# An encoder layer on one core: h's plain block through DRAM, T1 and T2 queued ahead, a tile pair of their own for w_down's first digits, the last store in halves

## The chip, the cores and the metric

The kernel runs on one core of one Trainium2 chip. The metric is the device time of one execution in microseconds (us); lower is better. Before the change three runs took 1528.82 to 1530.57 us, median 1529.31.

Engines are named as in the profile: PE is TensorE's matmul and PEld its weight load, DVE is VectorE, ACT is ScalarE, POOL is GpSimd, SP is SyncE, which here only issues DMAs. A DMA can be issued from ACT too (ACTq).

## The reference, cut to what matters

One layer on x of 1024 tokens by 1024 channels, all in float32:

```
h = rmsnorm(x, g_mix)
... pooling mixer and differential attention on h @ w_in, two gates ...
x = x + merged @ w_out
h2 = rmsnorm(x, g_ffn)
x = x + square(relu(h2 @ w_up)) @ w_down      # w_up: 1024 x 4096, w_down: 4096 x 1024
```

The change lies in the last three lines: the product with `w_out` (its end), the second norm, and the two products of the MLP.

## The kernel before

**Float32 out of three matmuls.** Every operand of a matmul is kept as two digits: `split` (L129-133) casts a block to hi on ACT (L131) and subtracts to get lo on DVE or POOL (L132). `mm3` (L135-140) then makes one product of 128 x 128 by 128 x 512 from three matmuls: hi x hi (L138), hi x lo (L139), lo x hi (L140).

**Seven products in place of eight.** The large products are cut into 2 x 2 blocks and done by a scheme of seven block products, named "1" to "7", with sums of blocks as operands. For w_up the token side is h2 transposed, in blocks B11, B21 (tokens 0 to 511, lower and upper half of the channels) and B12, B22 (tokens 512 to 1023). The operands are B11, B21, B22 and

```
T1 = B12 - B11      T2 = B22 - T1      T3 = B22 - B12      T4 = (B21 - B11) - T3
```

Each has a hi and a lo tile, filled in four column blocks of 128 tokens (t = 4 to 7). The profile names them BT1h, BT1l and so on; "t" is a block of T1 or T2 before the cast, "y" the block of h2 itself.

**End of the w_out stage, `first_half` (L1151-1159).** For tokens t = 0 to 3 the normed block is transposed on PE into two banks (hb) and split into B11 and B21. A plain copy of B11 (`r11`, ACT) is subtracted from B21, and the difference d21 is stored to DRAM (`nd`, SP), where T4 needs it later. r11 and d21 come from `tmp`, four slots in turn.

**The turn to the MLP, `second_half` and `combine` (L1272-1299).** For t = 4 to 7 the block is transposed and scaled by ACT (L1178) into `kept_b[t]`, which holds B12 and B22. T1 is made by two subtractions on DVE, B12 minus B11's hi and minus its lo; then T2 by one. T2 is split at once; T1, T3, B22 and T4 are split by four calls of `combine`, in this order. `combine("T3")` and `("22")` also work within y's room; for T4 the stored d21 is loaded back over B22 (L1297) once B22 is split.

**w_up, `up_pair` (L1332-1407).** Sixteen pairs p of column blocks; each pair has seven products of 12 matmuls: "1" on B11 into bank X, "2" on B21 into Y, then "6" (T2), "5" (T1), "7" (T3), "4" (T4), "3" (B22). The first products of pairs 0 to 3 run ahead during the turn. The second half of a pair's columns (`wu<p>_1`) is loaded into `pr20` or `pr21`; pr21 lies where the y blocks lay. The results go to DRAM (`ud`) as they are and in four sums us1 to us4 (udS), made last in each pair.

**w_down (L1458-1594).** Seven products of eight steps q; a step is 24 matmuls on two operands of 128 x 1024: `ur`, loaded back from ud, and a sum of blocks of w_down (`wd`, `wdt`). `operands` loads both and splits them into u_q and w_q. Those of product "1" for q = 0 to 2 are made early, beside the last pair; `t1_made(q)` makes T1 of w_down from `wdt` and gives back the tile of step q. At the end `finish_out` adds the bank to what was kept and stores four blocks of 128 x 512.

**What sets the order.** Each engine works through its own queue in order. The order of each queue isn't written by hand: a planner puts an instruction into its queue when, by its own estimates, its operands and its room are there, the most urgent by priority (`tc.cur_priority`) first. `tc.issue_after(x)` puts what is traced within it behind x in the queue of x's engine, without a wait. Waits are then added where data or a tile's bytes need them.

**Room.** Tiles are drawn from pools that are stacked from both sides of a partition, and pools of a later stage lie over closed ones of an earlier stage. The byte ranges per partition in the last two stages are these.

| w_up stage | bytes | w_down stage | bytes |
|---|---|---|---|
| wpool (cast w_up) | 18176-50944 | pwo (w digits) | 18176-50944 |
| hpT2, T1, T3, 22, T4 | 50944-132864 | pd (T1, T2, kept sums, residuals) | 50944-147200 |
| e1 (9 blocks: t, x1, U2, z5, U3, us) | 132864-151296 | prw1 (4 wd tiles) | 155392-171776 |
| es | 151296-155392 | pur1 (2 ur tiles) | 171776-179968 |
| e21 (s of other pairs) | 155392-163584 | puo (8 u digits) | 179968-212736 |
| pr21, e20, pr20 | 163584-179968 | prw0 (2 wd tiles) | 212736-220928 |
| pr1 (w_up) | 179968-196352 | pur0 (2 ur tiles) | 220928-229120 |
| nb (B11, B21) | 196352-229120 | | |

e1 itself lies over `rpool` and `fp` of the stage before it, where the raw w_out rows and `tmp`'s blocks are.

Of the kernel before, what the change touches and what calls it, by code (L numbers as in the profile page):

```python
# [8 lines left out]
F32 = mybir.dt.float32  # L9
# [8 lines left out]
P = 128  # L18
S = 1024
D = 1024  # L20
NT = S // P
# [42 lines left out]
def encoder_kernel(  # L64
# [21 lines left out]
    nc = tc.nc  # L86
    x, out = x[0], out[0]
# [5 lines left out]
    dram = ctx.enter_context(tc.tile_pool(name="dram", bufs=1, space=DRAM))  # L93
# [32 lines left out]
    def f(ap):  # L126
        return ap.bitcast(F32)

    def split(hi, lo, src, lo_eng=None):  # L129

        made = nc.scalar.copy(hi, src)  # L131
        (lo_eng or nc.vector).tensor_tensor(lo, src, f(hi), op=ALU.subtract)  # L132
        return made
# [264 lines left out]
    def fillers():  # L398
        gate_units = gates()
        for _ in range(G_FIRST):  # L400
            next(gate_units)
            yield
        for g in range(4):
            for _ in pool_group(g):
                yield
                next(gate_units)
                yield
        for _ in gate_units:
            yield
# [3 lines left out]
    with ExitStack() as ph:  # L413
# [83 lines left out]
        act, dve, pol = nc.scalar, nc.vector, nc.gpsimd  # L497
# [426 lines left out]
        units, made = fillers(), 0  # L924
# [29 lines left out]
    def add(eng, out_, a, b):  # L954
        eng.tensor_tensor(out_, a, b, op=ALU.add)

    def sub(eng, out_, a, b):
        eng.tensor_tensor(out_, a, b, op=ALU.subtract)

    dve, pool = nc.vector, nc.gpsimd  # L960
# [22 lines left out]
    def tmp(name):  # L983
        nbank[1] += 1
        return fr_tile([P, 512], name) if nbank[1] % 4 in (1, 2) else fo_tile(name)[:, 0:512]
# [22 lines left out]
    for d in range(NK):  # L1008
        if d % 2 == 0 and d + 2 < NK:
            ws_bp[d + 2] = load_cols2(w_branch_pool, (d + 2) * P, f"bp{d + 2}")  # L1010
        elif d > NK - 4:
            j = len(ws_ba)
# [126 lines left out]
    def norm_turn(t, bank_fn):  # L1139

        yn = y[t]
        ps = [bank_fn(j, f"hb{t}_{j}") for j in range(2)]
        for j, b in enumerate(ps):
            for i in range(4):
                k = 4 * j + i
                nc.tensor.transpose(b[:, i * P : (i + 1) * P], yn[:, k * P : (k + 1) * P], identf)
        return [b.rearrange("p (a b) -> p a b", a=4) for b in ps]

    nd = dram.tile([4, P, 4, P], F32, name="nd")

    def first_half(t):  # L1151
        b11, b21 = norm_turn(t, lambda j, name: o_bank(name, 2 * (t % 2) + j))
        b_split("11", t * P, b11, dve)
        b_split("21", t * P, b21, dve)

        r11, d21 = (tmp(f"{n}_{t}").rearrange("p (a b) -> p a b", a=4) for n in ("r11", "d21"))
        nc.scalar.copy(r11, b11)
        sub(dve, d21, b21, r11)
        nc.sync.dma_start(nd[t], d21)


    def o_bank(name, i):
        p, tag = ((ps_z, "z"), (ps_z, "z"), (ps_f, "f"), (pb, "b"))[i]
        return p.tile([P, 512], F32, tag=tag, name=name)

    kept_b, turned = {}, {}
# [6 lines left out]
    def second_turn(t, b):  # L1173
        kept_b[t] = y[t].rearrange("p (q a b) -> p q a b", q=2, a=4)
        for j in range(2):
            for i in range(4):
                k = 4 * j + i
                turned[t] = nc.scalar.activation(  # L1178
                    kept_b[t][:, j, i, :], b[j][:, i, :], AF.Copy, scale=cols[:, 21 + k : 22 + k]
                )  # L1180
# [47 lines left out]
    for step in O_TAIL.split():  # L1228
        t = int(step[1])
# [34 lines left out]
    def ev(name, shape=(P, 512)):  # L1264
        return e1.tile(list(shape), F32, tag="ev", name=name)
# [1 line left out]
    for q in ("T2", "T1", "T3", "22", "T4"):  # L1267
        Bq[q] = tuple(hpT[q].tile([P, 4, 512], F32R, tag="h", name=f"B{q}{i}") for i in "hl")

    T1s, T2_made = {}, {}  # L1270

    def second_half(t, after=None):  # L1272
        c0 = (t - 4) * P
        if after is not None:
            with tc.issue_after(after.ins):
                second_turn(t, norm_turn(t, lambda j, name: bm.tile([P, 512], F32, tag="ZW"[j], name=name)))
        t1, t2 = (ev(f"{n}_{t}", (P, 4, P)) for n in ("t1", "t2"))
        T1s[t] = t1
        cs = slice(c0, c0 + P)
        sub(dve, t1, kept_b[t][:, 0], f(Bq["11"][0][:, :, cs]))  # L1280
        sub(dve, t1, t1, f(Bq["11"][1][:, :, cs]))
        sub(dve, t2, kept_b[t][:, 1], t1)
        T2_made[t] = b_split("T2", c0, t2, dve)

    def combine(q):
        for t in range(4, NT):
            c0 = (t - 4) * P
            t3, b22 = kept_b[t][:, 0], kept_b[t][:, 1]
            if q == "T1":
                b_split(q, c0, T1s[t], dve)  # L1290
            elif q == "T3":
                sub(dve, t3, b22, t3)
                b_split(q, c0, t3, dve)
            elif q == "22":
                b_split(q, c0, b22, dve)
            else:
                nc.sync.dma_start(b22, nd[t - 4])  # L1297
                sub(dve, b22, b22, t3)
                b_split(q, c0, b22, dve)
# [14 lines left out]
    made = {}  # L1314
# [108 lines left out]
    for p, q in enumerate(("T1", "T3", "22", "T4")):  # L1423
        if p > 1:
            next(pairs[p])
        if q == "T3":
            body = tc.cur_priority

        with ExitStack() as later:
            if p:  # L1430
                later.enter_context(tc.issue_after(turned[NT - 1].ins))
            if q == "T4":
                later.enter_context(tc.issue_after(T2_made[NT - 1].ins))
            combine(q)
    norms.close()
    e2 = [pool_of(hs, "e20", 2, side="right")]
# [18 lines left out]

    purs = [pool_of(ctx, "pur0", 2, side="right")]  # L1458
    prws = [pool_of(ctx, "prw0", 2, side="right")]
    puo = pool_of(ctx, "puo", 8, side="right")  # L1460
# [3 lines left out]
    pwo = pool_of(ctx, "pwo", 8)  # L1464
# [4 lines left out]
    T1s, T2s = {}, {}  # L1469

    def kept(tag, q):
        return pd.tile([P, 2, 512], F32, tag=tag, name=f"{tag}_{q}", bufs=NQ)
# [4 lines left out]
    def quarter(j, q, ab, dh):  # L1477
        nraw[1] += j not in "1t"
        first = q % 4 < 2 if j == "1" else j != "t" and nraw[1] % 3 == 0
        r = prws[0 if first else 1].tile([P, 2, 512], F32, tag="rw", name=f"wd{j}_{q}_{ab}{dh}")  # L1480
        nc.sync.dma_start(r, wd[ab, :, q, :, dh * 512 : (dh + 1) * 512])
        return r

    def second(j, q):

        if j == "1":
            b11[q] = quarter(j, q, 0, 0)
            return b11[q]
        if j == "5":
            return T1s[q]  # L1490
        if j == "2":
            return quarter(j, q, 1, 0)
        if j == "3":
            return quarter(j, q, 1, 1)
        if j == "6":
            b22 = quarter(j, q, 1, 1)
            T2s[q] = kept("T2", q)
            sub(dve, T2s[q], b22, T1s[q])
            return T2s[q]
        if j == "7":  # L1500
            b22, b12 = quarter(j, q, 1, 1), quarter(j, q, 0, 1)
            sub(dve, b22, b22, b12)
            return b22
        b21 = quarter(j, q, 1, 0)
        sub(dve, b21, b21, T2s[q])
        return b21
# [3 lines left out]
    def t1_made(q):  # L1510
        b12 = quarter("t", q, 0, 1)
        T1s[q] = kept("T1", q)
        sub(dve, T1s[q], b12, b11.pop(q))

    def operands(j, q):
        nraw[0] += 1
        ur = purs[nraw[0] > 2 and nraw[0] % 2].tile([P, 2, 512], F32, tag="ur", name=f"ur{j}_{q}")
        nc.sync.dma_start(ur, ud[SIDES[j][0], q])
        out_ = []
        for n, src, pool_ in (("u", ur, puo), ("w", second(j, q), pwo)):  # L1520
            hi, lo = (pool_.tile([P, 2, 512], F32R, tag="op", name=f"{n}{j}_{q}{x}") for x in "hl")
            split(hi, lo, src, dve)
            out_ += [hi, lo]
        return out_

# [35 lines left out]
            got.append(k)  # L1561
        return got

    def finish_out(banks, parts, th, dh):
        for t in range(4):
            add(dve, parts[t], banks[t], parts[t])
            r0 = (4 * th + t) * P
            nc.sync.dma_start(out[r0 : r0 + P, dh * 512 : (dh + 1) * 512], parts[t])

    def four(tag):  # L1570
        return [bd.tile([P, 512], F32, tag=tag, name=f"D{tag}{t}", bufs=4) for t in range(4)]
# [16 lines left out]
    U3 = with_residual(DX, "U3y", 1, 0)  # L1588
# [2 lines left out]
    finish_out(DZ, U2, 0, 1)  # L1591
    DV = four("a")
    d_product(DV, "4", True)
    finish_out(DV, U3, 1, 0)


# [29 lines left out]
```

## Time and profile before

| | |
|---|---|
| three runs | 1529.31 us median, 1528.82 to 1530.57 |
| the profiled execution | 1529.07 us, of which the profile's span is 1527.3 |
| PE busy | 1518.3 us, 99% of the span, 7638 matmuls |
| DVE, ACT, POOL busy | 1018.6, 803.3, 357.6 us |
| DMA | 213.75 MB, mean 140 GB/s |
| granted TensorE clock | 1.00 |

The profile is one execution. Its span begins with the first recorded work and ends with the last; the 1.8 us between the span and the execution's time lie around it. A row of a timeline gives start and length in us, the engine, the line of the code, the operation, the output and the inputs, and in brackets how long the engine stood idle before it and what ended that. A matmul is shown with 0.39 us though the next starts 0.23 us later, since matmuls are pipelined; a PE that is "busy" can thus still lose time, which shows in the distance of starts. A row of busy time in a stretch gives, after the stretch, the busy us and the number of instructions of PE, PEld, DVE, ACT and POOL, then the granted clock, the DMA engines' busy share and GB/s. The row of a DMA issue ends with its size and the us from issue to landing. By time, w_out ends and the turn to the MLP begins at 905 us, w_up runs to 1217 and w_down to the end.

### The profile page before, as it was taken

How to read it: one execution, taken by the hardware profiler on the slowest of the kernel's cores; microseconds unless marked ns; L12 is line 12 of the kernel's file. 1: busy time of each engine (PE TensorE's matmuls, PEld its weight loads, DVE VectorE, ACT ScalarE, POOL GpSimd, SP SyncE). 2: the span in 40 equal slices, each digit the busy share in tenths (PEclk: the TensorE clock that was granted, in tenths of full speed). 3: DMA queues.
4: the chain of work that ended last, by engine and by line, in shares of the span. 5: the costliest groups of instructions: out<-in, count | busy, mean ns of one | idle time of the engine just before them, and what ended most of it. 6: DMA issues, size and time to landing. Idle time of an engine off the chain costs nothing.

```text
span 1527.3 us, 21610 instructions
## 1 busy us (share of the span) xinstructions
PE 1518.3 (99%) x7638; PEld 1316.7 (86%) x7638; DVE 1018.6 (67%) x2073; ACT 803.3 (53%) x1653; POOL 357.6 (23%) x403
## 2 busy tenths in 40 slices
PE   9999999999999999999999999999999999999999
PEld 8999999999999999888888887888888788888887
DVE  7777766677676777642745899676656678556572
ACT  6656565556565655544633467565555634333331
POOL 4424142424233342227736510000000000000000
PEclk9999999999999999999999999999999999999999
DMA  6212121111212021339845633554432899537750
GB/s 219 65 44 66 36 63 38 59 52 47 62 36 75 31 90 49 118 108 357 280 144 176 211 137 118 173 193 159 152 124 110 290 332 365 185 125 262 225 194 28
DMA packets 168583, 213.75 MB, mean 140 GB/s; under 512 B 10165, under 2 KB 104090, under 8 KB 168474
## 3 DMA queue, kind: packets, MB, share of 16 engines
q1 hardware_dynamic: 151050, 185.05, 36.6%
q10 hardware_dynamic: 17424, 27.31, 4.8%
q8 instruction: 60, 0.98, 0.3%
q14 instruction: 49, 0.40, 0.1%
HBM read 154.62 MB, written 57.70 MB: 139 GB/s over the span
## 4 chain that ended last, share of the span: by engine, by line
PE 93%; DVE 4%; DMA 1%; ACT 1%; issue 1%; SPq 0%; POOLq 0%; POOL 0%; ACTq 0%; DVEq 0%
PE z L138 6%; PE z L140 6%; PE z L139 6%; PE Da L139 4%; PE Da L140 4%; PE g L139 4%; PE Da L138 4%; PE g L140 4%; PE g L138 4%; PE Db L140 3%; PE Db L138 3%; PE Db L139 3%; PE X L138 3%; PE X L140 3%; PE X L139 3%; PE sc L774 2%
## 5 line engine op out<-in xcount | busy, mean ns | idle before, releaser
L138 PE MATMUL z<-wqkv,hT 128*128 128x384 f32 x512 | 174.2, 341 | 0.1
L140 PE MATMUL z<-wqkv,hT 128*128 128x384 f32 x512 | 174.0, 340 | 0.3 <-DVE hT L437 0.3
L139 PE MATMUL z<-wqkv,hT 128*128 128x384 f32 x512 | 173.1, 338 | 0.0
L785 ACT ACTIVATE s<-s,nm 128x256 f32<-128x256 f32 (+7 forms) x128 | 99.5, 778 | 73.3 <-DVE nm L777 72.6
L708 POOL TENSOR_TENSOR ms<-ms,mhalf 128x4 f32<-128x4 f32 x64 | 70.6, 1103 | 210.3 <-DVE ms L707 207.1
L139 PE MATMUL g<-hT,fwgate 128*128 128x512 f32 x256 | 100.7, 394 | 0.0
L138 PE MATMUL g<-hT,fwgate 128*128 128x512 f32 x256 | 100.7, 393 | 0.0
L140 PE MATMUL g<-hT,fwgate 128*128 128x512 f32 x256 | 100.5, 394 | 0.0
L138 PEld LDWEIGHTS z<-wqkv,hT 128*128 128x128 f32 x512 | 96.2, 188 | 3.3 <-ACT hT L437 0.4
L139 PEld LDWEIGHTS z<-wqkv,hT 128*128 128x128 f32 x512 | 96.3, 188 | 2.5 <-DVE wqkv L437 0.3
L140 PEld LDWEIGHTS z<-wqkv,hT 128*128 128x128 f32 x512 | 96.2, 188 | 2.5 <-DVE hT L437 0.8
L777 DVE CUSTOM_DVE_ANT_0 s<-sc,dist 128x512 f32<-128x512 f32 (+3 forms) x128 | 74.6, 586 | 22.9 <-PE sc L775 21.7
L774 PE MATMUL sc<-K,Q 128*128 128x512 f32 (+2 forms) x192 | 67.6, 356 | 0.1
L775 PE MATMUL sc<-K,Q 128*128 128x512 f32 (+2 forms) x192 | 65.7, 348 | 0.0
L132 DVE TENSOR_TENSOR AS<-s,AS 128x512 fp32r<-128x512 f32 x64 | 43.4, 687 | 32.4 <-ACT AS L131 32.3
L132 POOL TENSOR_TENSOR wqkv<-rqkv,wqkv 128x384 fp32r<-128x384 f32 x56 | 58.1, 1062 | 11.8 <-ACT wqkv L131 11.3
L132 POOL TENSOR_TENSOR fwgate<-frgate,fwgate 128x512 fp32r<-128x512 f32 x32 | 44.5, 1392 | 69.1 <-ACT fwgate L131 69.1
L140 PEld LDWEIGHTS g<-hT,fwgate 128*128 128x128 f32 x256 | 48.1, 188 | 9.6
L139 PEld LDWEIGHTS g<-hT,fwgate 128*128 128x128 f32 x256 | 48.1, 188 | 9.0 <-DVE hT L132 0.3
L138 PEld LDWEIGHTS g<-hT,fwgate 128*128 128x128 f32 x256 | 48.1, 188 | 8.8 <-ACT hT L131 0.3
L132 DVE TENSOR_TENSOR AT_0l<-ta,AT_0h 128x512 fp32r<-128x512 f32 (+1 forms) x48 | 32.0, 666 | 30.9 <-ACT AT_0h L131 30.4
L138 PE MATMUL ba<-yT,wba 128*128 128x512 f32 x128 | 49.8, 389 | 0.0
(484 smaller groups left out, 4583.6 us busy)
## 6 DMA issues: line engine op xcount, KB each, us to landing
wd<-in_w_down_dram SPq DMA_DIRECT2D x56, 512.0 KB, 5.5
wu<-in_w_up_dram SPq DMA_DIRECT2D x32, 512.0 KB, 4.3
udS<-us SPq DMA_DIRECT2D x64, 256.0 KB, 3.4
ur<-udS SPq DMA_DIRECT2D x32, 512.0 KB, 5.3
rqkv<-in_w_in_dram SPq DMA_DIRECT2D x64, 192.0 KB, 2.7
ur<-ud SPq DMA_DIRECT2D x24, 512.0 KB, 5.7
frgate<-in_w_gate_dram SPq DMA_DIRECT2D x32, 256.0 KB, 3.8
g_dram<-go ACTq DMA_DIRECT2D x32, 256.0 KB, 2.5
```

The lines of the kernel that those rows point to most:

```text
L132: (lo_eng or nc.vector).tensor_tensor(lo, src, f(hi), op=ALU.subtract)
L138: nc.tensor.matmul(ps, lhs_hi, rhs_hi, start=first, stop=False, **kw)
L139: nc.tensor.matmul(ps, lhs_hi, rhs_lo, start=False, stop=False, **kw)
L140: return nc.tensor.matmul(ps, lhs_lo, rhs_hi, start=False, stop=last, **kw)
L708: nc.gpsimd.tensor_tensor(ms, ms, mhalf[:, 0:4], op=ALU.pow)
L774: nc.tensor.matmul(dst, Q[:, i, 0, :], rhs, start=True, stop=False)
L775: nc.tensor.matmul(dst, Q[:, i, 1, :], rhs, start=False, stop=True)
L777: nc.vector.tensor_tensor_reduce(out=s[i][:, c : c + w], in0=sc[:, 0:w], in1=dist[:, o0 + c : o0 + c + w], scale=2.0 ** -(h + 1), scalar=B ...
L785: nc.scalar.activation(s[i][:, 0:n], s[i][:, 0:n], AF.Exp, bias=last, scale=-1.0, accum_out=Z[:, i, t : t + 1])
```

## The change

- **nr.** `first_half` also stores r11, the plain block of B11, to DRAM (`nr`, SP). Before the turn four loads bring the blocks back into the tiles that will be T1. T1 is then one subtraction, B12 minus the loaded block, in place of two.
- **Order.** What `combine` casts for T3, B22 and T4 is now queued on ACT behind the casts of the last block (t = 7) of T2 and of T1; before, it was queued behind the last turned block, and T4 behind T2 too.
- **pw0.** A pool of two tiles (8 KB), opened first on the right side, takes the two digits w_0 of product "1"; all others stay in pwo. The ACT casts of u and w for q = 2 and 3 of product "1" are queued behind w_0's cast.
- **Last store.** The last block of the last product is added and stored in two halves of 256 columns, the first store on SP, the second on ACT.

```diff
-    nd = dram.tile([4, P, 4, P], F32, name="nd")
+    nd, nr = (dram.tile([4, P, 4, P], F32, name=n) for n in ("nd", "nr"))
...
         nc.scalar.copy(r11, b11)
+        nc.sync.dma_start(nr[t], r11)
         sub(dve, d21, b21, r11)
...
-    T1s, T2_made = {}, {}
+    T1s, T2_made, T1_made = {}, {}, {}
+    for t in range(4, NT):
+        T1s[t] = ev(f"t1_{t}", (P, 4, P))
+        nc.sync.dma_start(T1s[t], nr[t - 4])
...
-        t1, t2 = (ev(f"{n}_{t}", (P, 4, P)) for n in ("t1", "t2"))
-        T1s[t] = t1
-        cs = slice(c0, c0 + P)
-        sub(dve, t1, kept_b[t][:, 0], f(Bq["11"][0][:, :, cs]))
-        sub(dve, t1, t1, f(Bq["11"][1][:, :, cs]))
+        t1, t2 = T1s[t], ev(f"t2_{t}", (P, 4, P))
+        sub(dve, t1, kept_b[t][:, 0], t1)
         sub(dve, t2, kept_b[t][:, 1], t1)
...
             if q == "T1":
-                b_split(q, c0, T1s[t], dve)
+                T1_made[t] = b_split(q, c0, T1s[t], dve)
...
             if p:
-                later.enter_context(tc.issue_after(turned[NT - 1].ins))
-            if q == "T4":
                 later.enter_context(tc.issue_after(T2_made[NT - 1].ins))
+                later.enter_context(tc.issue_after(T1_made[NT - 1].ins))
             combine(q)
...
+    pw0 = pool_of(ctx, "pw0", 2, side="right")
     purs = [pool_of(ctx, "pur0", 2, side="right")]
...
+        first = (j, q) == ("1", 0)
+        for n, src, pool_ in (("u", ur, puo), ("w", second(j, q), pw0 if first else pwo)):
             hi, lo = (pool_.tile([P, 2, 512], F32R, tag="op", name=f"{n}{j}_{q}{x}") for x in "hl")
-            split(hi, lo, src, dve)
+            with tc.issue_after(first_w[0].ins) if j == "1" and 1 < q < 4 else nullcontext():
+                made = split(hi, lo, src, dve)
+            if first:
+                first_w[0] = made
...
+            n = 256 if last and t == 3 else 512
+            for c in range(0, 512, n):
+                add(dve, parts[t][:, c : c + n], banks[t][:, c : c + n], parts[t][:, c : c + n])
+                (nc.scalar if c else nc.sync).dma_start(
+                    out[r0 : r0 + P, dh * 512 + c : dh * 512 + c + n], parts[t][:, c : c + n]
+                )
```

With pw0 at 220928-229120 the pools opened after it on the right lie 8 KB lower: pur0 212736-220928, prw0 204544-212736, puo 171776-204544, pur1 163584-171776, prw1 147200-163584.

More of the change, by code (lines that the diff above doesn't have):

```diff
@@ L1513, in t1_made @@
         sub(dve, T1s[q], b12, b11.pop(q))
+    first_w = [None]
     def operands(j, q):
@@ L1519, in operands @@
         out_ = []
-        for n, src, pool_ in (("u", ur, puo), ("w", second(j, q), pwo)):
+        first = (j, q) == ("1", 0)
+        for n, src, pool_ in (("u", ur, puo), ("w", second(j, q), pw0 if first else pwo)):
             hi, lo = (pool_.tile([P, 2, 512], F32R, tag="op", name=f"{n}{j}_{q}{x}") for x in "hl")
-            split(hi, lo, src, dve)
+            with tc.issue_after(first_w[0].ins) if j == "1" and 1 < q < 4 else nullcontext():
+                made = split(hi, lo, src, dve)
+            if first:
+                first_w[0] = made
             out_ += [hi, lo]
@@ L1562, in with_residual, with finish_out @@
         return got
-    def finish_out(banks, parts, th, dh):
+    def finish_out(banks, parts, th, dh, last=False):
         for t in range(4):
-            add(dve, parts[t], banks[t], parts[t])
             r0 = (4 * th + t) * P
-            nc.sync.dma_start(out[r0 : r0 + P, dh * 512 : (dh + 1) * 512], parts[t])
+            n = 256 if last and t == 3 else 512
[4 more added lines that the diff above has]
+                )
     def four(tag):
@@ L1593, in encoder_kernel @@
     d_product(DV, "4", True)
-    finish_out(DV, U3, 1, 0)
+    finish_out(DV, U3, 1, 0, True)
 _INS = [
```

## The prediction

> **What bounds the kernel now.** I read the page first, then the busy time in chosen stretches, the waits of PE, and the timelines of single engines around the three places where PE stands.
>
> ```profile
> span 1527.3 us, 21610 instructions
> PE 1518.3 (99%) x7638; PEld 1316.7 (86%) x7638; DVE 1018.6 (67%) x2073; ACT 803.3 (53%) x1653; POOL 357.6 (23%) x403
> 930.00:940.00 10.00, 8.67 (x37) 6.59 (x36) 10.00 (x18) 8.80 (x17) 0.00 (x0) 1.00 0.68 210
> 940.00:950.00 10.00, 9.55 (x43) 7.57 (x42) 6.98 (x13) 4.91 (x10) 0.00 (x0) 1.00 0.43 132
> 1215.00:1220.00 5.00, 4.29 (x18) 2.94 (x17) 3.98 (x5) 3.89 (x7) 0.00 (x0) 1.00 0.72 248
> 1300.00:1500.00 200.00, 200.00 (x884) 165.60 (x883) 118.22 (x112) 74.21 (x74) 0.00 (x0) 1.00 0.57 185
> 1520.00:1527.30 7.30, 3.52 (x16) 2.59 (x14) 1.38 (x2) 0.00 (x0) 0.00 (x0) 1.00 0.23 90
> ```
>
> PE is busy in 1518.3 of 1527.3 us, at a granted clock of 1.00. No matmul goes, so the change can only win from the 9.0 us in which PE stands, and what lies within its reach is small: 1.33 + 0.45 us at 930 to 950, 0.71 at 1215 to 1220, and the 3.8 us tail. In steady work a matmul starts every 200 / 884 = 0.226 us; PE's losses are better read from its starts than from its busy time:
>
> ```profile
> 931.83 0.39 PE L138 MATMUL Z<-BT1h,AS 128*128 128x512 f32 x1
> 933.23 0.50 PE L138 MATMUL X<-BT2h,AS 128*128 128x512 f32 x1 [1.00 <-ACT BT2h L131]
> 934.05 0.50 PE L139 MATMUL Z<-BT1l,AS 128*128 128x512 f32 x1 [0.32 <-DVE BT1l L132]
> 941.93 0.39 PE L138 MATMUL W<-BT4h,A 128*128 128x512 f32 x1
> 942.77 0.50 PE L138 MATMUL X<-BT3h,AS 128*128 128x512 f32 x1 [0.45 <-ACT U L1376]
> ...
> 1217.18 0.39 PE L140 MATMUL Z<-B22h,AS 128*128 128x512 f32 x1
> 1218.21 1.21 PE L138 MATMUL Da<-w_0h,u_0h 128*128 128x512 f32 x4 [0.64 <-ACT w_0h L131]
> 1219.49 0.50 PE L139 MATMUL Da<-w_0l,u_0h 128*128 128x512 f32 x1
> ```
>
> Place A, 930 to 943: starts come 1.40, 0.82 and 0.84 us apart instead of 0.23, which loses 1.17 + 0.59 + 0.61 = **2.4 us**. Place B, the start of w_down: 1.03 - 0.23 = 0.80, and the lo digit is late by 1219.49 - (1218.21 + 4 x 0.226) = 0.37, together **1.17 us**. Place C is the tail.
>
> **Part 1 and 2: T1 from nr, and the casts of T1 and T2 ahead.** They meet at place A. What PE waits for there is late on ACT and DVE:
>
> ```profile
> L958 DVE TENSOR_TENSOR t<-t,B11l x4: 677/684/692, 906.5 to 925.5; 128x512 f32<-128x512 f32 x4
> 903.00:942.00 39.00, 37.67 (x181) 30.82 (x179) 38.12 (x70) 33.35 (x81) 3.17 (x3) 1.00 0.28 95
> 923.24 1.67 ACT L1178 ACTIVATE y<-hb,cols 128x128 f32<-128x128 f32 x6
> 924.74 1.72 ACT L131 CAST BT3h<-y 128x512 fp32r<-128x512 f32 x3
> 926.82 1.72 ACT L131 CAST B22h<-y 128x512 fp32r<-128x512 f32 x3
> 930.47 0.67 ACT L131 CAST BT1h<-t 128x512 fp32r<-128x512 f32 x1
> 932.50 0.67 ACT L131 CAST BT2h<-t 128x512 fp32r<-128x512 f32 x1
> 940.52 1.89 DVE L132 TENSOR_TENSOR BT4l<-y,BT4h 128x512 fp32r<-128x512 f32 x3
> DMA to landing us min/median/max: 2.6/2.6/2.6
> ```
>
> The last turned block of h is there at 924.9, but six casts of T3 and B22 pass the last T1 and T2, which are cast at 930.5 and 932.5. The change queues them behind. After 924.9 come two subtractions (starts 0.60 us apart, as three take 1.89), two casts of 0.5 and two lo digits: all four by about 928. PE needs them at 931.8, so this wait goes with 3 us to spare. Four subtractions of 0.60 go from DVE, which is busy in 38.1 of the 39 us up to 942: 2.4 us. Added are four stores and four loads of 256 KB on SP; the nearest row is nd, 2.6 us to land each. The stores lie beside the nd stores and no slot of `tmp` is asked for again within that time. The loads cannot be queued before the `tmp` pool under e1 is given back; its last store is issued at 903.3 by the first row below and lands 2.6 later, so the first plain block is back at about 908.5, where T1's second subtraction now starts at 906.5. DVE has other work then; I let it lose 0 to 1 us.
>
> ```profile
> 900.58 3.03 SPq L1159 DMA_DIRECT2D nd<-d  x2
> 941.24 14.30 SPq L1340 DMA_DIRECT2D wu<-in_w_up_dram  x5
> 945.44 0.69 DVE L955 TENSOR_TENSOR s<-wu 128x512 f32<-128x512 f32 x1 [3.02 <-DMA wu<-in_w_up_dram]
> ```
>
> What is late next is T4. Its second lo digit, the first of the three at 940.52, frees the y block into which pair 1's w_up columns are loaded (issued at 941.24, used at 945.44). Without the waits PE has done pair 0's five other products, and the one of pair 4 that its timeline shows between them, by 931.8 + 6 x 12 x 0.226 = 948.1, and then wants pair 1. T3, B22 and T4 are now queued later, but DVE has up to 2.4 us less to do before them, so I expect that load 1.4 to 2.4 us earlier, and pair 1's sums, casts and digits with it. I take **-1.9 us**; the ends are -2.4 (all of place A) and -0.6 (B22 is cast 2 us later, nd's 2.6 us stand behind it, and only part is won back).
>
> **Part 3: w_down's first digits.** They get pw0, 8 KB over the pool of B11 and B21, whose last reader is pair 15's second product; five products of 12 x 0.226 = 2.7 us follow it, so it is free before 1204. The data are asked for ahead of the wd load at 1194.99 below and land in 5.5 us, so hi and lo can be made ten us early, and both halves of place B go: **-1.17 us**. But 8 KB at the right edge push every later right-hand pool down by 8 KB. That matters because the planner hands a pool's room on as a whole, which three pairs of rows show:
>
> ```profile
> 1194.27 0.69 DVE L132 TENSOR_TENSOR AS<-s,AS 128x512 fp32r<-128x512 f32 x1 [3.11 <-ACT AS L131]
> 1194.99 0.38 SPq L1481 DMA_DIRECT2D wd<-in_w_down_dram  x1
> ...
> 1207.39 0.69 DVE L132 TENSOR_TENSOR AS<-s,AS 128x512 fp32r<-128x512 f32 x1
> 1208.11 0.82 SPq L1518 DMA_DIRECT2D ur<-ud  x2
> ...
> 1222.56 3.39 SPq L1359 DMA_DIRECT2D udS<-us  x4
> 1226.04 1.36 SPq L1552 DMA_DIRECT2D x1y<-yd  x3
> 1218.22 1.22 DVE L132 TENSOR_TENSOR w_0l<-wd,w_0h 128x1024 fp32r<-128x1024 f32 x1
> 1221.63 1.04 ACT L131 CAST w_2h<-wd 128x1024 fp32r<-128x1024 f32 x1
> wd<-in_w_down_dram SPq DMA_DIRECT2D x56, 512.0 KB, 5.5
> wu<-in_w_up_dram SPq DMA_DIRECT2D x32, 512.0 KB, 4.3
> ```
>
> prw1's first load leaves at 1194.99, as the last digit out of e21 ends (1194.96); pur1's first when e20's ends, at 1208.08; pd's first behind the last store out of e1. After the change puo covers e20 and pr20, so the casts of u_0 to u_3 move behind 1208.1: four casts of 1.04 and four lo digits of 1.22 (w_2h and w_0l have their shape) fit before 1217.4 beside what ACT and DVE do for pair 15, and cost nothing. prw1 comes to lie at 147200 to 163584, over the top 4 KB of e1 and all of es. Its first tile is q = 2 of product "1", now loaded at 1195; it will be queued behind pair 15's four us stores.
>
> When is that? The stores go out from 1222.56 to 1225.95 now, after w_0's cast and digit (1.04 and 1.22 us) have stood ahead of pair 15's last steps on ACT and DVE; without them they go 0 to 2.3 us earlier, so the load leaves between 1223.7 and 1226.0. It lands 4.3 (wu's median) to 5.5 us later (wd's), and the cast takes 1.04. PE wants q = 2 at 1217.41 + 48 x 0.226 = 1228.3. Early ends: 1223.7 + 4.3 + 1.04 = 1229.0, a stall of 0.7; late ends: 1226.0 + 5.5 + 1.04 = 1232.5, a stall of 4.2. I take 1.8, nearer the early end, since DMA then has fewer loads before it. Behind it q = 3 lands one or two loads later and is wanted 24 x 0.226 = 5.4 us later, so it follows in time. Part 3 in sum: -1.17 + 1.8 = **+0.6**, ends -1.2 and +3.0.
>
> **Part 4: the last store.**
>
> ```profile
> 1523.56 0.69 DVE L955 TENSOR_TENSOR U3y<-Da,U3y 128x512 f32<-128x512 f32 x1 [2.03 <-PE Da L140]
> 1525.00:1526.00 1.00, 0.00 (x0) 0.00 (x0) 0.00 (x0) 0.00 (x0) 0.00 (x0) 1.00 0.68 262
> L132 DVE TENSOR_TENSOR hT<-hps,hT 128x256 fp32r<-128x256 f32 x20 | 7.5, 414 | 3.2 <-ACT hT L131 3.0
> ```
>
> The 256 KB move in 0.68 us, after which nothing runs but the landing; half takes 0.34. A read of PSUM with 256 columns takes 414 ns, so two adds in a row, overlapping by 0.09 as others do, end some 0.05 to 0.14 us after the one of 0.69. The second half leaves from ACT, whose issue no row of the tail shows: at best it costs what SP's does, at worst one issue more, 0.82 / 2 = 0.41 us by the row of two above. I take **-0.2**, ends -0.3 and +0.2. [...]
>
> **Sum.** -1.9 + 0.6 - 0.2 = -1.5 us. The profiled execution took 1529.07 (span 1527.3 and 1.8 around it), 0.24 under the median 1529.31; so 1527.6 against the one and 1527.8 against the other, and I say **1527.7**. A measurement of this kernel can tell about 0.2% (3.06 us) from no change.
>
> **Rivals.**
> - The handover of prw1 costs nothing (the load goes out by tile, or its slots are empty early). For: data are asked for 20 us ahead at all other places. Against: the three pairs of rows. -2.4 - 1.17 - 0.3 = -3.9: 1525.2. Chance 0.27; these are the faster cases.
> - Place A moves instead of going: pair 1's load or the T4 digits hold PE at 948 instead. For: pair 1's load waits for T4, which is now queued last. Against: from the load's landing to PE's want there are over 4 us for two sums, a cast and a digit. -0.6 + 0.6 - 0.2: 1528.9. Or the planner still makes w_0 late and nothing is won at B. Chance 0.15.
> - Slower: q = 2's load also waits for the landing of the last us store (1226.0 + 2.6) and then takes the median 5.5 us: 1234.1 + 1.04, and 0.3 more for the lo digit, is 7.1 us late. -1.9 - 1.17 + 7.1 - 0.2 = +3.8: 1532.9. It decides from a load issued at 1227.8 on. For: the last 4 KB of e1 may well hold one of the us blocks. Against: four of its nine, and the us steps come earlier. Chance 0.11.
>
> The forecast has 0.47. Faster by over 0.2%: 0.27; within: 0.62; slower: 0.11. The range runs from 1525.0, all gains and no new wait, to 1531.2, with most of the late load in it.
>
> **What will show it.** Right: BT1h and BT2h cast before BT3h, no wait of PE for them; Da's first matmul 0.23 us after the last Z; a wait of PE for w_2h some 11 us later; prw1's first wd load next to the us stores. Wrong: that load before 1210, or a PE wait near 948 above 1 us, or T1's loads holding DVE for more than 1 us at 906.

## The result, and the profile after

The change makes the kernel slower: 1540.32 us median of six runs (1538.97 to 1542.12) against 1529.26 of six runs of the kernel before, a ratio of 1.0071 [1.0058, 1.0084]. The forecast was 1527.7, range 1525.0 to 1531.2. The profiled execution took 1538.97 us, 9.9 more than the one of before, and is the fastest of the six.

From the page of the changed kernel, and from its waits of PE (waiting tile and releaser; us in total, times, longest):

```profile
span 1537.2 us, 21623 instructions
PE 1521.3 (99%) x7638; PEld 1317.8 (86%) x7638; DVE 1018.7 (66%) x2070; ACT 804.4 (52%) x1653; POOL 357.3 (23%) x403
```

```profile
PE Da L138 <- ACT w_2h L131: 3.0, 1, 3.0
PE X L138 <- ACT AS L131: 2.5, 1, 2.5
PE Db L138 <- ACT w_0h L131: 1.9, 1, 1.9
PE W L138 <- ACT A L131: 0.8, 1, 0.8
```

The page alone hides the loss: PE still shows 99%. These waits lie at three places (X and W are one place), and none of them is in the list of the kernel before. The same stretches as before, with the granted clock after the five engines' busy times:

```profile
930.00:940.00 10.00, 9.56 (x43) 7.58 (x41) 10.00 (x17) 8.79 (x18) 0.00 (x0) 1.00 0.52 149
940.00:950.00 10.00, 8.46 (x36) 6.68 (x36) 6.59 (x12) 4.80 (x10) 0.00 (x0) 1.00 0.59 193
950.00:960.00 10.00, 8.06 (x26) 5.72 (x27) 10.00 (x18) 6.03 (x11) 0.00 (x0) 0.83 0.53 161
1215.00:1220.00 5.00, 5.00 (x24) 4.14 (x23) 2.74 (x3) 1.95 (x3) 0.00 (x0) 1.00 0.84 270
1300.00:1500.00 200.00, 200.00 (x884) 165.62 (x883) 122.58 (x116) 73.50 (x74) 0.00 (x0) 1.00 0.60 203
```

930 to 940 and 1215 to 1220 are fuller than before, as meant; from 1300 on the rate is the same (884 matmuls in 200 us). What is lost is lost in 945 to 1275.

**Place A, the turn.** PE in the kernel before, and in the changed one:

```profile
950.63 0.39 PE L140 MATMUL Z<-B22h,AS 128*128 128x512 f32 x1
950.85 0.39 PE L138 MATMUL X<-BT2h,AS 128*128 128x512 f32 x1
```

```profile
948.19 0.39 PE L140 MATMUL W<-BT4h,A 128*128 128x512 f32 x1
951.06 0.50 PE L138 MATMUL X<-BT2h,AS 128*128 128x512 f32 x1 [2.49 <-ACT AS L131]
953.14 0.50 PE L138 MATMUL W<-BT4h,A 128*128 128x512 f32 x1 [0.82 <-ACT A L131]
```

The matmul of 948.19 is, counted in order, the one of 950.63 before: 2.44 us earlier. Not all of that is won here. The changed trace is ahead by 0.76 us already at 904, from the first 30 us of the kernel, where nothing was changed; some 1.7 us are won at place A, and the waits for BT1 and BT2 are gone. Then pair 1 isn't there, and its first matmul starts 0.21 later than before. After the wait for A the granted clock is 0.50 from 953.64 to 957.06. At the last matmul of w_up (1217.18 before, 1220.56 now) PE is 3.38 us late, so place A lost 3.38 + 0.76 = 4.1 us. Why pair 1 is late is seen on DVE (the last row is one of the kernel before), SP and ACT:

```profile
906.29 0.22 DVE L1130 TENSOR_SCALAR nrs<-nss 128x1 f32<-128x1 f32 x1 [0.81 <-ACT y L1123]
907.43 0.88 DVE L1137 TENSOR_SCALAR y<-mp,nrs 128x512 f32<-128x512 f32 x2 [0.73 <-POOL nrs L271]
909.15 0.69 DVE L958 TENSOR_TENSOR t<-y,t 128x512 f32<-128x512 f32 x1 [0.84 <-DMA t<-nr]
919.49 0.88 DVE L1137 TENSOR_SCALAR y<-mp,nrs 128x512 f32<-128x512 f32 x2 [0.44 <-POOL nrs L271]
947.87 0.69 DVE L955 TENSOR_TENSOR s<-wu 128x512 f32<-128x512 f32 x1 [2.25 <-DMA wu<-in_w_up_dram]
949.68 0.68 DVE L958 TENSOR_TENSOR s<-s,wu 128x512 f32<-128x512 f32 x1
```

```profile
946.65 0.68 DVE L958 TENSOR_TENSOR s<-s,wu 128x512 f32<-128x512 f32 x1
```

```profile
905.74 1.88 SPq L1274 DMA_DIRECT2D t<-nr  x4
943.84 8.12 SPq L1341 DMA_DIRECT2D wu<-in_w_up_dram  x3
```

```profile
930.23 0.67 ACT L131 CAST BT2h<-t 128x512 fp32r<-128x512 f32 x1
930.75 1.71 ACT L131 CAST BT3h<-y 128x512 fp32r<-128x512 f32 x3
950.39 1.14 ACT L131 CAST AS<-s 128x512 fp32r<-128x512 f32 x2
```

The plain blocks are asked for at 905.74 and T1's first subtraction runs at 909.15, where DVE has stood 0.81 + 0.73 + 0.84 = 2.38 us: about what the four saved subtractions were worth (4 x 0.60). Only the last of the three gaps is ended by a load; the other two are ended by ACT and POOL within the norm, and the kernel before ran T1's two subtractions at 905.73 and 906.48, in that stretch. The last block's norm is written at 919.49 (917.34 before). BT3h begins at 930.75 (924.74 before), behind BT2h; pair 1's load leaves at 943.84 (941.24 before) and its first sum is made at 947.87 (945.44). Product "6", the first that PE wants, takes the second sum (`s<-s,wu`), which is made of the first. DVE runs it at 949.68 (946.65 before), 0.6 later behind the first than before, since another add (`U<-Z,U`) comes in between; its cast begins as soon as it ends, at 950.39.

**Place B, the start of w_down**, on PE, SP and DVE:

```profile
1220.56 0.39 PE L140 MATMUL Z<-B22h,AS 128*128 128x512 f32 x1
1220.79 0.39 PE L138 MATMUL Da<-w_0h,u_0h 128*128 128x512 f32 x1
1234.81 1.20 PE L138 MATMUL Da<-w_2h,u_2h 128*128 128x512 f32 x4 [2.98 <-ACT w_2h L131]
```

```profile
1225.74 2.25 SPq L1360 DMA_DIRECT2D udS<-us  x4
1228.80 0.32 SPq L1521 DMA_DIRECT2D ur<-ud  x1
1229.21 0.39 SPq L1482 DMA_DIRECT2D wd<-in_w_down_dram  x1
```

```profile
1227.55 1.22 DVE L132 TENSOR_TENSOR u_4l<-ur,u_4h 128x1024 fp32r<-128x1024 f32 x1
```

w_down starts 0.23 us behind w_up's last matmul, without a wait. w_2's load leaves at 1229.21, behind the us stores and behind a ur load whose tile is read by u_4l until 1228.77. PE gets to q = 2 at 1220.79 + 48 x 0.226 = 1231.6 and its first matmul starts at 1234.81, 3.2 late; the lo digit costs some 0.5 more.

**A third place, the start of product "2"**, where the kernel before waits for nothing. ACT and PE:

```profile
1267.95 1.04 ACT L131 CAST u_3h<-ur 128x1024 fp32r<-128x1024 f32 x1 [4.38 <-PE Da L139]
1268.90 1.04 ACT L131 CAST w_0h<-wd 128x1024 fp32r<-128x1024 f32 x1
```

```profile
1267.75 0.39 PE L140 MATMUL Da<-w_7h,u_7l 128*128 128x512 f32 x1
1269.99 1.19 PE L138 MATMUL Db<-w_0h,u_0h 128*128 128x512 f32 x4 [1.85 <-ACT w_0h L131]
```

w_0 is cast behind u_3, which waits until PE has read the old tile with its last matmuls of Da. The starts are 2.24 apart: 2.0 lost, some 0.4 at the lo digit, and then the granted clock is 0.50 again, from 1271.08 to 1274.49.

**The clock.** The following rows of the changed kernel are cut at steps of 3.413 us, the length of each stretch at 0.50, counted from 953.64, where the first begins:

```profile
950.23:953.64 3.41, 1.75 (x6) 0.90 (x6) 3.41 (x7) 3.40 (x7) 0.00 (x0) 1.00 0.15 39
953.64:957.06 3.42, 3.36 (x9) 2.46 (x8) 3.42 (x7) 1.77 (x3) 0.00 (x0) 0.50 0.69 233
1230.12:1233.53 3.41, 1.71 (x8) 1.09 (x6) 0.81 (x1) 1.04 (x1) 0.00 (x0) 1.00 1.00 340
1233.53:1236.95 3.42, 2.08 (x8) 1.41 (x9) 2.57 (x3) 1.62 (x2) 0.00 (x0) 1.00 1.05 403
1267.66:1271.08 3.42, 1.56 (x7) 0.72 (x5) 3.25 (x5) 3.13 (x4) 0.00 (x0) 1.00 0.90 314
1271.08:1274.49 3.41, 3.15 (x8) 2.47 (x8) 3.41 (x4) 1.73 (x2) 0.00 (x0) 0.50 1.00 371
```

Within the span the granted clock is 0.50 in exactly two of these windows, each the one after a window with few matmuls (x6 and x7, where a full one has 16 or 17: x16 from 957.06 to 960.47, x17 in the kernel before from 927.99 to 931.40). In the first of the two, matmuls start 0.43 us apart (954.61 to 956.32) instead of 0.226. Each window costs half of 3.413, **1.71 us**, as an estimate from that length and the clock of 0.50.

The ledger of the profiled execution, by starts of the same matmuls in the two traces: -0.8 in the first 30 us, outside the change; +4.1 at A (with one window of half clock); -1.3 at the start of w_down; +3.7 at w_2 (3.2 + 0.5); +4.1 at product "2" (2.0 + 0.4 + 1.7). The last matmul starts at 1532.97 instead of 1523.13, 9.8 later.

### The profile page after: what moved, and what is told of

It is laid out like the page before. It is cut to its first block, busy times and chain, and to the rows that moved or that the text cites. A ratio compares the mean times of both kernels' runs of the same rounds, so it can differ in the third digit from the quotient of the medians.

```text
span 1537.2 us, 21623 instructions
## 1 busy us (share of the span) xinstructions
PE 1521.3 (99%) x7638; PEld 1317.8 (86%) x7638; DVE 1018.7 (66%) x2070; ACT 804.4 (52%) x1653; POOL 357.3 (23%) x403
## 4 chain that ended last, share of the span: by engine, by line
PE 91%; DVE 4%; DMA 2%; ACT 1%; issue 1%; SPq 0%; POOLq 0%; POOL 0%; ACTq 0%; DVEq 0%
PE z L140 6%; PE z L138 6%; PE z L139 6%; PE Da L139 4%; PE g L140 4%; PE g L139 4%; PE Da L140 4%; PE g L138 4%; PE Da L138 4%; PE Db L139 3%; PE Db L140 3%; PE Db L138 3%; PE X L140 3%; PE X L138 2%; PE X L139 2%; PE sc L774 2%
```

## The experiments

The theory after the two traces: A is lost to the order of part 2, all behind 1217 to part 3; the rivals blame the loads of part 1, and for product "2" the shift of time. Each kernel is given with its median, its runs, and its ratio to the kernel before on the same chip.

**One part alone, four kernels.** Each is the kernel before with that part of the diff above.

*Part 1 alone.*

> The kernel before with part 1 alone: T1 in one subtraction from the stored plain block, and T3, B22 and T4 queued as before. Theory: the order, not the loads, made pair 1 late, so here no wait of PE above 1 us near 948 and no half clock behind it; T1(7) and T2(7) stay behind T3 and B22, so the two waits at 930 to 934 shrink at most: 1527 to 1529.5 us. Rival: the loads of the plain block made DVE idle at 906 to 910 and that made T4 and pair 1's load late: a wait of PE above 1 us near 948, the clock halved for 3.4 us after it, 1531 to 1533.

1530.43 us (10 runs), ratio 1.0008 [0.9998, 1.0017]. Nothing is gained, and no wait near 948; but in the profile the waits at 930 to 934 grow, 0.9 for BT1h and 1.5 for BT2h, where they were to shrink. DVE stands 0.81, 0.73 and 0.66 us at 907 to 910, as in the changed kernel. The profiled execution is by far the slowest of the ten (1534.79; the others 1529.42 to 1531.31): behind these waits two windows of half clock follow (0.50 from 934.79 to 941.62), which neither theory nor rival named.

*Part 2 alone.*

> The kernel before with part 2 alone: T3, B22 and T4 queued behind the last casts of T2 and T1, T1 still by two subtractions. Theory (order): T3, B22 and T4 come later by about as much as in the changed kernel or more, since DVE has 2.4 us more to do: pair 1's w_up load leaves after 943, PE waits 2.5 to 5 us for pair 1 near 950, the clock is halved once for 3.4 us: 1531.5 to 1535 us. Rival (loads): without the plain block's loads the order costs nothing and the waits at 930 to 934 go: 1526.9 to 1528.5.

1528.91 us (10 runs), ratio 0.9997 [0.9987, 1.0007]: the theory's 1531.5 to 1535 was wrong. The waits at 930 to 934 are gone, and their place is taken by one for pair 1. SP and PE:

```profile
942.38 8.51 SPq L1340 DMA_DIRECT2D wu<-in_w_up_dram  x3
```

```profile
949.39 0.50 PE L138 MATMUL X<-BT2h,AS 128*128 128x512 f32 x1 [1.55 <-ACT AS L131]
```

The load is 1.1 us later than before, and PE waits 1.55 and 0.49 us. In the profiled execution (1530.15) one window of half clock follows (0.50 from 951.46 to 954.87), as the theory had it; seven of the ten runs have a mean clock of 1.000 and a median of 1528.71. The order moves place A and, by the runs, neither wins nor loses.

*Part 3 alone.*

> The kernel before with part 3 alone: w_0's tile pair in pw0, the casts of u and w of q = 2 and 3 behind w_0's. Theory: all that the changed kernel lost after 1217 comes from it: 1.2 won at the start of w_down, 3.3 lost to the late w_2, 2.2 lost at the start of product 2 and 1.7 to the halved clock there: +6.0, 1535 us (1533.5 to 1536.5). Rival: the loss at the start of product 2 belongs to the shift of time by the turn or to DMA traffic that happened to meet there; then it is absent here: 1.2 won, 3.3 lost, 1531.4.

1534.7 us (5 runs), ratio 1.0033 [1.0019, 1.0046], in the theory's range, but not by its sum. In the profiled execution, the slowest of the five (1535.89), the starts fall back by 2.1 us at place A, which this kernel doesn't change (1.7 of it, by the estimate above, a window of half clock, 0.50 from 935.23 to 938.64), gain 1.3 at the start of w_down and lose 6.1 at w_2, where another such window follows:

```profile
1234.37 1.19 PE L138 MATMUL Da<-w_2h,u_2h 128*128 128x512 f32 x4 [3.84 <-ACT w_2h L131]
```

```profile
1235.60:1239.01 3.41, 3.38 (x8) 2.71 (x9) 3.22 (x3) 1.04 (x1) 0.00 (x0) 0.50 1.03 336
```

Product "2" starts without a wait, so that loss isn't part 3's alone.

*Part 4 alone.*

> The kernel before with part 4 alone: the last block added and stored in halves, the second store from ACT. Theory: from the last matmul's start to the span's end 4.17 us before and 4.2 in the changed kernel, so nothing won or lost: 1529.3 (1528.7 to 1530), tail 4.1 to 4.3. Rival: in the changed kernel the tail was lengthened by chance and the smaller transfer wins its 0.2 to 0.3: tail 3.85 to 4.0.

1529.25 us (10 runs), ratio 1.0003 [0.9994, 1.0012]; from the last matmul's start to the span's end 4.2 us, as in the changed kernel. No difference.

**Parts 1 and 2 together.**

> The kernel before with parts 1 and 2 together, without 3 and 4. Alone each left the time as it was; theory: together they do not, since the plain block's loads make the last tokens' norm and turn some 2 us late, and the order then puts T3, B22, T4 and pair 1's w_up load behind it. A wait of PE of 2 to 3 us near 950 for pair 1 and, mostly, one window of half clock behind it; starts of matmuls after 956 lie 2 to 3.7 us later than before: 1531 to 1533.5 us. Rival: what the changed kernel lost at 950 needs part 3 too, or was a chance of the clock: 1528.5 to 1530 us, wait below 1.6 us as with the order alone.

1531.09 us (10 runs), ratio 1.0009 [1.0000, 1.0018], at the lower edge of the theory's range. In the profiled execution, one of the fastest (1530.00), PE waits 1.5 and 0.8 us for pair 1 and its matmuls then start 1.0 us later than before, without a window of half clock (1.00 from 947.46 to 957.70); six of the ten runs have a mean clock of 0.998 or 0.999. So a loss is there, at the edge of what these runs can tell, and smaller than the 4.1 us of the changed kernel. Here T1's first subtraction doesn't wait for its load (908.44, against 909.15), and pair 1's load leaves at 942.73 instead of 943.84; why the loads land in time here and not there stays open.

**Parts 1 and 2, the stored block for tokens 6 and 7 only.**

```diff
-    for t in range(4, NT):
+    for t in range(6, NT):
         T1s[t] = ev(f"t1_{t}", (P, 4, P))
         nc.sync.dma_start(T1s[t], nr[t - 4])
...
```

Of the stored blocks only the two that are loaded remain, and T1 of tokens 4 and 5 is made by two subtractions as before.

> Parts 1 and 2 as in the kernel with both, but only T1 of tokens 6 and 7 comes from the stored plain block; T1 of tokens 4 and 5 takes two subtractions again. Theory: with both parts pair 1 comes late because DVE stands 2.4 us at 906 to 909 for the first loads, which pushes the norm and turn of token block 7 by 2 us; here block 7's norm is back at 917.5 (919.5 with both), pair 1's w_up load leaves at 942 or before (943.8 in the changed kernel), PE waits at most 1.5 us near 950: 1528.5 to 1530. Rival: the plain block's loads and stores hold DMA or SP up, or DVE's work itself is the limit: load at 943 or later, 1530.5 to 1532.

1529.51 us (10 runs), ratio 1.0000 [0.9991, 1.0009]. The last block's norm is at 918.27, between the 917.34 of the kernel before and the 918.78 with all four blocks; the load leaves at 942.16 (942.73 with all four). PE's waits near 950 sum to 2.1, over the 1.5 expected, and its matmuls then start as late as before: this is the order alone again. That the loads for tokens 4 and 5, the first that T1 needs, are what part 1 costs is likely by the 1.0 us between the two traces; the two ratios' intervals overlap, so it isn't shown.

**Part 3 with prw1 in two pools of two tiles.**

```diff
-    prws.append(pool_of(ctx, "prw1", 4, side="right"))
+    prws += [pool_of(ctx, n, 2, side="right") for n in ("prw1", "prw2")]
+    nr1 = [0]
...
-        r = prws[0 if first else 1].tile(
+        nr1[0] += not first
+        r = prws[0 if first else 1 + (nr1[0] - 1) % 4 // 2].tile(
...
```

> The kernel before with part 3 alone, but prw1's four tiles in two pools of two, filled in the same turn, so that only the last two lie over e1 and es. Theory (room handed on as a whole): w_2's load goes back to about 1195 and w_2 is cast long before it is wanted; no wait of PE at 1230, 1.2 won at the start of w_down: 1528 to 1529 us. Rival (part 3 is late for another reason, such as the casts of u moved behind 1208 or the order behind w_0's cast): w_2's cast still late, a wait above 1 us near 1230: 1531 to 1535.

1529.83 us (10 runs; one of them took 1885 us and isn't in the ratio), ratio 1.0003 [0.9993, 1.0013]. w_2 isn't waited for, and w_down starts 1.3 us better; but PE now waits 0.92 us for w_1 of product "2", and by starts loses 1.7 there. So the room of the pool made w_2 late; the gain is given back 45 us on.

**The changed kernel with prw1 in two pools.** The same edit.

> The changed kernel with prw1's four tiles in two pools of two, as in the split version before, and nothing else. Theory: of the changed kernel's +11 us, the late w_2 (3.3) and what follows it at the start of product 2 (2.2) and one or two windows of half clock (1.7 each) go; the loss at 950 stays: 1532 us (1530.5 to 1533.5), no wait above 1 us after 1217. Rival: the start of product 2 is late because of the whole change's shift and the full DMA engines, not because of the room: a wait above 1 us near 1268 stays, 1534 to 1537.

1533.37 us (10 runs), ratio 1.0019 [1.0009, 1.0028], inside the theory's range: by the ratios eight of the eleven us go. One wait of 1.0 (w_1) stays at product "2", at the bound that was set; w_0 isn't waited for, and by starts 1.8 us are lost there instead of 4.1. In its profile pair 1 is late by 2.7 us and two windows of half clock follow (0.50 from 950.29 to 957.12). So the room as a whole costs the changed kernel more than w_2: much of the loss at product "2" goes with it.

**The changed kernel with w_0 of product "2" cast ahead of u_3.**

```diff
...
+            behind = first_w[0] if j == "1" and 1 < q < 4 else first_2[0] if (j, q) == ("2", 3) else None
-            with tc.issue_after(first_w[0].ins) if j == "1" and 1 < q < 4 else nullcontext():
+            with tc.issue_after(behind.ins) if behind is not None else nullcontext():
                 made = split(hi, lo, src, dve)
+            if (j, q, n) == ("2", 0, "w"):
+                first_2[0] = made
...
```

> The changed kernel with one order more: u_3's cast of product 2 queued behind w_0's. Theory: at 1268 PE waits only because w_0's cast stands behind u_3's on ACT, which waits until PE has read u_3's old tile; without it the wait of 1.85 goes, with the lo digit's 0.3 and the half clock's 1.7: 1536.4 (1535.3 to 1537.5). Rival: w_down's loads are late there (DMA engines busy all the time), the cast waits for DMA instead: wait above 1 us, 1539 to 1541.

1537.5 us (4 runs), ratio 1.0049 [1.0032, 1.0066]. The time is near the theory's, the reason isn't: PE still waits 1.42 us there, now for the load.

```profile
1270.44 1.04 ACT L131 CAST w_0h<-wd 128x1024 fp32r<-128x1024 f32 x1 [4.90 <-DMA wd<-in_w_down_dram]
```

ACT stood 4.9 us with nothing ahead of w_0. The cast order explains 0.4 of the 1.85; the rest is a late load. The profiled execution is the slowest of the four (1538.92) and its last matmul starts only 0.05 us before that of the changed kernel: it has no half clock behind product "2" (from 1273.13 on its matmuls start 0.23 us apart), but one behind w_2, 0.50 from 1236.84 to 1240.25. Where the loads went shows in the stretch ahead of w_down, kernel before, changed kernel and part 3 alone (the last two numbers are the DMA engines' busy share and GB/s):

```profile
1190.00:1217.00 27.00, 27.00 (x121) 22.36 (x120) 14.92 (x21) 15.76 (x25) 0.00 (x0) 1.00 0.97 336
```

```profile
1190.00:1217.00 27.00, 27.00 (x121) 22.37 (x120) 16.72 (x23) 16.04 (x26) 0.00 (x0) 1.00 0.65 232
```

```profile
1190.00:1217.00 27.00, 27.00 (x121) 22.34 (x120) 15.91 (x22) 15.31 (x25) 0.00 (x0) 1.00 0.68 233
```

27 us x 104 GB/s = 2.8 MB, some five loads of 512 KB, are no longer moved there; four are loads of w_down (six leave between 1190 and 1197 before, two now), and they come after 1229, where the share is 1.0 in the rows above. But they can't be the whole reason for the late product "2": part 3 alone moves the same loads, and there w_0 is cast at 1265.57, 3.5 us before PE wants it (1269.10). So it takes the moved loads, as the two pools show, and something of the other parts; which, isn't shown. Why the whole change puts w_0 behind u_3 on ACT, where part 3 alone keeps the order of before, lies in the planner's estimates and stays open too.

**T4 in T1's tile.** Since the order alone only moves place A to pair 1's load, that load was freed: nd goes into T1's tile, which is read for the last time by T1's lo digit, and no longer over B22; y's room then comes free when T4's difference is made.

```diff
-                nc.sync.dma_start(b22, nd[t - 4])
-                sub(dve, b22, b22, t3)
-                b_split(q, c0, b22, dve)
+                t4 = T1s[t]
+                nc.sync.dma_start(t4, nd[t - 4])
+                sub(dve, t4, t4, t3)
+                b_split(q, c0, t4, dve)
```

With part 2, and with part 3 in the two pools:

> A version made of what the runs say: part 2 (order) without part 1, nd loaded into T1's tile instead of over B22 so that T4 waits for neither B22's digits nor frees y late, part 3 with prw1 in two pools; no halves. Theory: pair 1's w_up load leaves 1.5 us or more earlier than with the order alone (942.4), the 2.4 us at 930 to 943 and the 1.2 us at 1217 go without a new wait: 1525.7 (1524.5 to 1527.3). Rival: the blocks of e1 that T1 and T4 hold longer, or the nd loads, hold up pair 0 or 1 by as much: 1528 to 1530.

1527.11 us (10 runs), ratio 0.9985 [0.9976, 0.9994]: a little faster than the kernel before, in the theory's range. By starts w_down begins 1.3 us better here, and product "2" gives 1.3 back.

With part 2 alone, nothing of parts 1, 3 and 4:

> The kernel before with part 2 (order) and nd loaded into T1's tile for T4; nothing of parts 1, 3, 4. Theory: all that the version with T4 in T1's tile won comes from the turn: the waits of 2.4 us at 930 to 943 gone and no wait for pair 1: matmuls after 956 start 2 to 2.5 us earlier than before, and with fewer windows of half clock 1527 us (1526.3 to 1527.9). Rival: half of it came from the tile pair pw0: 1528 to 1528.8.

1527.15 us (11 runs, 1526.28 to 1528.05), ratio 0.9982 [0.9973, 0.9990]. As much as with part 3, so it came from the turn. SP, and the busy time in place A:

```profile
912.14 13.23 SPq L1298 DMA_DIRECT2D t<-nd  x3
...
937.85 14.77 SPq L1341 DMA_DIRECT2D wu<-in_w_up_dram  x5
```

```profile
930.00:940.00 10.00, 10.00 (x45) 8.28 (x45) 10.00 (x17) 9.60 (x19) 0.00 (x0) 1.00 0.41 117
940.00:950.00 10.00, 9.55 (x42) 7.57 (x41) 10.00 (x18) 5.96 (x12) 0.00 (x0) 1.00 0.51 156
```

Three of the four nd loads leave from 912 on, pair 1's load 3.4 us earlier than before, and PE has one wait of 0.4 left. This version beats both kernels.

The first of these two once more, with u_3 and u_4 of product "2" cast behind its w_1, the order of the kernel before:

> The version with T4 in T1's tile, the order and the split room, and besides u_3 and u_4 of product 2 cast behind its w_1, which stood there in the kernel before and not in the split version. Theory: the wait of 0.5 to 0.9 us for w_1 at 1267 was the ACT order's: it goes, 1526.2 (1525.5 to 1527). Rival: w_1's load is late there, since DMA is full: the wait stays, 1527 to 1527.6.

1528.48 us (11 runs), ratio 0.9988 [0.9979, 0.9997]. The wait for w_1 shrinks to 0.2, but the runs aren't faster than without it, and by starts product "2" still loses 1.0: the expected 1526.2 was wrong.

## Why the prediction failed, point by point

- **Parts 1 and 2, taken at -1.9: wrong in sign, +4.1 by starts.** Right was that BT1h and BT2h pass BT3h and are no longer waited for. The step that failed is "DVE has up to 2.4 us less to do before them, so I expect that load 1.4 to 2.4 us earlier": it came 2.6 us later. One error is in part 1: the loads were let cost DVE "0 to 1 us", on the ground that it has other work, but in the order that the planner chose it had none, stood 2.38 us, and the last norm fell back by 2.2. The other is in part 2: the order alone makes the load 1.1 us later, since T3, B22, nd's load, T4 and pair 1 hang on one another and all start behind T2. The prediction had the mechanism as its rival "Place A moves" and set it aside with "over 4 us" between the load's landing and PE's want. Those 4 us come out only with the load 1.4 us or more earlier (948.1 - 945.44 + 1.4 = 4.1): the argument against the rival rested on the step that failed. With the load where it was they are 2.7; as it came, the first sum starts 0.5 before PE wants its product (947.87, 948.41).
- **Part 3, the gain of 1.17: right** (1.3 by starts), with w_0's digits made early; Da starts 0.23 behind Z.
- **Part 3, the late w_2: right in mechanism, the term mis-sized.** The load left at 1229.21, which is 1225.8 with the 3.38 us of place A taken off, inside the stated 1223.7 to 1226.0, and the 3.7 us lost (3.2 and the lo digit's 0.5) lie inside 0.7 to 4.2; 1.8 was taken, nearer the early end. So part 3's sum was +2.4 up to there, not +0.6. The us stores were gone at 1228.0; the load left 1.2 later, behind a ur load in SP's queue. The slower rival (a wait for the last landing and then a load of 5.5) didn't happen: w_2's cast began 4.5 after its load left. The kernel with two pools shows that the room is the cause.
- **Product "2": not in the prediction.** "Behind it q = 3 lands one or two loads later ... so it follows in time" looked one step ahead, and there it was right: q = 3 isn't waited for. The term that was put at nothing is the next product, where 4.1 us were lost. The changed kernel with prw1 in two pools loses 1.8 there, and part 3 alone nothing; so the room and something of the other parts meet, and how they do stays open.
- **Part 4, taken at -0.2: nothing.** On DVE:

```profile
1533.39 0.76 DVE L955 TENSOR_TENSOR U3y<-Da,U3y 128x256 f32<-128x256 f32 x2 [2.03 <-PE Da L140]
```

  The two adds take 0.76 instead of 0.69; the second store leaves ACT at 1534.18, and from the last matmul's start to the span's end it is 4.2 us in both. With a half store, 0.34 us less to move by the prediction's reckoning, the kernel ended no sooner.
- **The clock: not in the prediction.** It treated a wait as worth its length. Two waits cost 1.71 us more each in the profiled execution, by the estimate above, and these 3.4 us are within the terms above. Four of the other five runs of the changed kernel have a lower mean clock than its 0.998 (0.994 or 0.995) and take 1.2 to 3.2 us longer.
- **The signs named in advance.** "A PE wait near 948 above 1 us" came, with 2.49. "T1's loads holding DVE for more than 1 us" came only if the whole stand of 2.38 is counted; the gap that a load's landing ended is 0.84. They point at the two errors of place A. The signs of being right came as well: the matmul behind the last Z, w_2h waited for, its load next to the us stores.
- **Together.** Against the forecast of -1.5 the profiled execution is off by 6.0 at place A, 1.8 at the start of w_down and w_2, 4.1 at product "2" and 0.2 at the tail, less the 0.8 of the first 30 us: 11.3 us. Of the rivals only "Place A moves" named a mechanism that happened, and it took -0.6 for the place, not +4.1.

## What to carry to other kernels

When a wait is taken away, what is late next must be measured against the new, earlier time at which PE arrives, and a chain that is queued behind the rescued instruction starts later (here BT3h by 6.0 us, at 930.75 instead of 924.74); if nothing shortens that chain, the wait only moves. It paid to free the load at its end (T4 in a tile of its own). A pool opened at the edge shifts every pool behind it: look at which early loads lose their room, and at how full the DMA engines are where those loads will go instead (here a share of 1.00 from 1230.12 to 1233.53).

## What the hardware showed

In the changed kernel the granted clock falls from 1.00 to 0.50 for whole windows on a fixed grid: the two within its span are 3.413 us long and begin at 953.64 and 1271.08, 317.44 us or 93 x 3.4133 apart. It goes with the window before. In the rows above x6 and x7 matmuls are followed by half clock and x8 and x8 aren't, and so it is in all whole windows within the spans of this kernel and of the kernel before: none above x7 is followed by half clock. The windows read in the other traces agree: at full clock, x7 (part 1 alone), x5 (part 2), x6 and x4 (part 3), x6 (the changed kernel with prw1 in two pools), x4 and x6 (with w_0 of product "2" ahead of u_3) were each followed by 0.50; x8 in part 3 alone and x8 in both kernels of parts 1 and 2 were followed by 1.00. A wait of 2.98 us that the grid cut into two windows cost no clock (1.00 from 1230.12 to 1236.95), one of 1.85 inside a single window did (0.50 from 1271.08).

In the kernel before, place A fills such a window to x8:

```profile
931.40:934.81 3.41, 2.08 (x8) 1.21 (x7) 3.41 (x7) 2.96 (x7) 0.00 (x0) 1.00 0.90 251
```

The next window, to 938.22, is at 1.00 with x16. With the same place in another position on the grid (part 3 alone, 931.82 to 935.23) six matmuls are left and the next window is at 0.50. That would let the same kernel run in two times, and its runs fit: of the 33 beside the last four kernels, 15 have a mean clock of 1.000 and a median of 1529.45 us, 18 have 0.999 and 1531.2. On the two other chips 6 of 26 have 0.999 (1530.34 against 1529.36) and 9 of 25 (1531.00 against 1528.98). None of these slower executions was profiled, so that it is place A that trips them is argued, not shown. With T4 in T1's tile and the order, 10 of 11 runs have 1.000, and the eleventh, the profiled one, has 0.999, with 1.00 from 930 to 960; where its clock is lower isn't shown. (Such a window elsewhere counts in the mean too, so the split isn't exact.)
